# A macaron decoder layer: splitting the FFN's hidden tiles in the output projection, and 15 instead of 12 of 22 pairs as seven block products

## The chip, the cores and the metric

The kernel runs on one core of a Trainium2 chip. The metric is the device time of one execution in microseconds.

## The reference

One layer over 512 tokens of width 1024, all in float32, with four residual sub-layers in order: a half-step SwiGLU FFN, a token mixer (a gated delta rule and a sparse attention in parallel), a second half-step FFN, and a gated per-layer embedding. The change lies in the two FFNs, which compute

```
def swiglu(u, w_in, w_out):                  # u: 512 x 1024
    gate, up = split(u @ w_in, 2)            # w_in: 1024 x 5632, gate and up: 512 x 2816
    return (silu(gate) * up) @ w_out         # w_out: 2816 x 1024

h = h + 0.5 * rmsnorm(swiglu(rmsnorm(h, g_pre), w_in, w_out), g_post)
```

## The kernel before, in words

**Precision.** Each float32 operand is held as two tiles, a rounded hi part and a lo part (the value less its hi part). `mm3` (line 99) issues three matmuls for a product: hi x hi, hi x lo, lo x hi. A hi part is made by ScalarE (a cast), a lo part by VectorE (a subtraction). `wchunk` (line 83) loads a weight tile of 128 x 1024 through SP's queue and makes both parts; `parts` (line 282) does so for a tile that is already there.

**Input projection of an FFN** (`ffn`, line 384). The 2816 hidden channels are 22 tiles of 128 (f = 0 to 21), each with a gate and an up weight tile, a *pair*. The first pairs (f = 0 to 2 in the first FFN, 0 and 1 in the second) are done in two halves of 256 tokens by `start_tiles`. Of the rest, a *direct* pair makes two `pgu` tiles of 128 channels x 512 tokens: 8 steps over the width times 3 matmuls each, 48 matmuls of 512 columns. `ev` takes the gate through Silu (ScalarE, line 395), multiplies by up (VectorE, 398) and makes hid's hi and lo part (399, 400).

The other pairs go through `Seven.pair` (line 333): the pair is a 2 x 2 block product (gate and up by the two halves of the width, the two halves of the width by the two halves of the tokens) made with seven block products in place of eight, of the kind of Strassen and Winograd. The sums of token blocks are made once per FFN (`Seven.__init__`, after f = 3). For each pair VectorE makes sums of weight blocks (sa, sb; lines 339 to 343), `parts` splits three operands x1, x2, x3 of 128 x 1024 and one, x4, of 128 x 512, and TensorE does seven products of 12 matmuls of 256 columns: x1 twice, x2, x3, x2, x4, x3. They stand in four PSUM tiles (pfa, pfb, pfc, pfd), which lines 367 to 377 add up in the tile c; Silu (379), product (380) and the split into hid (382) follow.

The operands take turns in a ring of four slots (`ring`, line 320): three of the tags whi/wlo, and one, xr, at every fourth request. The raw weights take turns in four buffers (`load`, line 326), whether the pair is direct or not. x4, sa and sb have one buffer each.

Before, the pairs with f of at least 4 that are no multiple of 3 are sevens: 4, 5, 7, 8, ..., 19, 20, 12 in all, two at a time with a direct pair behind them.

**Output projection** (`out_proj`, line 188). Two halves of the output columns (ch), each with four accumulators (acc, one for each 128 tokens). For each half the loop runs over 11 weight tiles (j), each of which takes hid tiles 2j and 2j + 1: 4 x 2 x 3 matmuls of 512 columns. `load` (line 438) fetches the weights of j; the first two of ch = 0 take whi/wlo slots, the others the two buffers of vhi/vlo (which hold two of the sums of u before). The residual for the end (hr) is loaded on SP's queue into the buffer hz, which holds the other sums of u until the last seven.

**Order.** Each engine runs its instructions in an order fixed when the kernel is built: a scheduler simulates the program and gives each engine the ready instruction that stands first in the program. An engine can so be given work from further down the program when its buffers are free.

Of the kernel before, what the change touches and what calls it, by code (L numbers as in the profile page):

```python
# [7 lines left out]
F32 = mybir.dt.float32  # L8
F32R = mybir.dt.float32r
AF = mybir.ActivationFunctionType  # L10
ALU = mybir.AluOpType
# [4 lines left out]
T = 512  # L16
# [16 lines left out]
def layer_kernel(ctx, tc, x, pT, wf1, wo1, wfm, wsm, wtm, wbr, wout, wf2, wo2, wgate, wproj,  # L33
                 gains, consts, params, out):
    nc = tc.nc
    V, A, G, PE, SY = nc.vector, nc.scalar, nc.gpsimd, nc.tensor, nc.sync
# [4 lines left out]
    sp = ctx.enter_context(tc.tile_pool(name="sp", bufs=2))  # L41
# [14 lines left out]
    def mmp(name="mm"):  # L56
        return pp_.tile([128, 512], F32, name=name, tag="mm")

    def axp(name="ax"):
        return pp_.tile([128, 512], F32, name=name, tag="ax")  # L60
# [19 lines left out]
    def gain_row(i):  # L80
        return bass.AP(tensor=gains.tensor, offset=gains.offset + i * D, ap=[[0, 128], [1, D]])
# [17 lines left out]
    def mm3(ps, l, r, start, stop):  # L99
        PE.matmul(ps, l[0], r[0], start=start, stop=False)  # L100
        PE.matmul(ps, l[0], r[1], start=False, stop=False)  # L101
        return PE.matmul(ps, l[1], r[0], start=False, stop=stop)  # L102

    def cols(pair, a, b):
        return pair[0][:, a:b], pair[1][:, a:b]
# [7 lines left out]
    def new_u():  # L113
        return (up.tile([128, KT, T], F32R, name="uhi"), up.tile([128, KT, T], F32R, name="ulo"))

    def u_at(u, k, n):
        return u[0][:, k, n], u[1][:, k, n]
# [133 lines left out]
    def start_tiles(tiles, u):  # L251

        for si, n in enumerate(SEG):
            for i, (w, r, ev) in enumerate(tiles):
                ps = (mmp if si == 0 else axp)("p0")
                with in_order() if env.puts else ExitStack():
                    for k in range(KT):
                        m = mm3(ps[:r, n], cols(w, k * r, (k + 1) * r), u_at(u, k, n), k == 0, k == KT - 1)
                ev(n, ps)
                if si == 0 and i:  # L260
                    put(i + 1, m)
# [20 lines left out]
    def parts(dst, src):  # L282
        A.copy(dst[0], src)  # L283
        V.tensor_sub(dst[1], src, dst[0].bitcast(F32))
        return dst

    class Seven:
# [45 lines left out]
        def pair(self, f, wg, wu, hid):  # L333
            g, w = self.load(wg), self.load(wu)
            sa = env.small.tile([128, 1024], F32, name="sa", tag="gp")
            sb = env.small.tile([128, 1024], F32, name="sb", tag="gn")
            x4 = lp.tile([128, 1024], F32R, name="x4", tag="gx")
            x1 = parts(self.ring(), g)
            V.tensor_tensor(sa[:, H1], w[:, H1], w[:, H2], op=ALU.add)
            V.tensor_tensor(sa[:, H2], sa[:, H1], g[:, H1], op=ALU.subtract)  # L340
            x2 = parts(self.ring(), sa)
            V.tensor_tensor(sb[:, H1], g[:, H1], w[:, H1], op=ALU.subtract)
            V.tensor_tensor(sb[:, H2], g[:, H2], sa[:, H2], op=ALU.subtract)
            x3 = parts(self.ring(), sb)
            x4 = parts((x4[:, H1], x4[:, H2]), w[:, H2])
            N1, N2 = SEG

            def product(ps, x, c, b):
                for k in range(4):
                    mm3(ps, cols(x, c + k * 128, c + k * 128 + 128), b(k), k == 0, k == 3)  # L350

            def tb(i):
                return lambda k: (self.t[i][0][:, k], self.t[i][1][:, k])

            def ub(k0, n):
                return lambda k: u_at(self.u, k0 + k, n)

            def two(ps):
                return ps.rearrange("p (a b) -> p a b", b=256)

            def bc(a):
                return a[:, None, :].to_broadcast([128, 2, 256])

            c = self.fp.tile([128, 4, 256], F32, name=f"ct{f}", tag=f"hid{f}")
            pa, pb, pc, pd = mmp("pfa"), axp("pfb"), mmp("pfc"), axp("pfd")
            product(pa[:, N1], x1, 0, ub(0, N1))
            A.copy(c[:, 0], pa[:, N1])
            product(pb[:, N1], x1, 512, ub(4, N1))
            product(pb[:, N2], x2, 512, tb(1))
            V.tensor_tensor(c[:, 1:3], two(pb), bc(c[:, 0]), op=ALU.add)  # L370
            product(pc[:, N1], x3, 0, tb(2))
            product(pc[:, N2], x2, 0, tb(0))
            V.tensor_tensor(c[:, 0::3], two(pc), bc(c[:, 2]), op=ALU.add)
            V.tensor_tensor(c[:, 2], pc[:, N2], c[:, 0], op=ALU.add)
            product(pd[:, N1], x4, 0, tb(3))
            product(pd[:, N2], x3, 512, ub(4, N2))
            V.tensor_tensor(c[:, 0::3], two(pd), c[:, 0::3], op=ALU.add)
            t = sp.tile([128, 2, 256], F32, name="gt", tag="t512", bufs=2)
            A.activation(t, c[:, 1::2], AF.Silu)
            V.tensor_tensor(t, t, c[:, 0::2], op=ALU.mult)  # L380
            hid[f] = self.fp.tile([128, 2, T], F32R, name=f"hid{f}")
            parts((hid[f][:, 0], hid[f][:, 1]), t.rearrange("p a b -> p (a b)"))

    def ffn(fp, free, wf, wo, hsrc, u, gi, gn_i, first):
        hid = [None] * FT
        g = {}

        def ev(f, part):
            def run(n, ps):
                if part == 0:  # L390
                    if f == 2 and len(first) == 6:
                        t = g[f] = lp.tile([128, T + 608], F32, name="gx")
                    else:
                        t = g[f] = sp.tile([128, T], F32, name="gt", tag="t512", bufs=2)
                    A.activation(t[:, n], ps[:, n], AF.Silu)
                else:
                    t = g[f]
                    V.tensor_tensor(t[:, n], ps[:, n], t[:, n], op=ALU.mult)
                    A.copy(hid[f][:, 0, n], t[:, n])
                    V.tensor_sub(hid[f][:, 1, n], t[:, n], hid[f][:, 0, n].bitcast(F32))  # L400
            return run

        def hid_tile(f):
            return fp.tile([128, 2, T], F32R, name=f"hid{f}")

        nf = len(first) // 2
        for f in range(nf):
            hid[f] = hid_tile(f)
        start_tiles([(w, 128, ev(i // 2, i % 2)) for i, w in enumerate(first)], u)
        seven = None  # L410
        for f in range(nf, FT):
            if f >= 4 and f % 3:
                seven.pair(f, wf[2 * f], wf[2 * f + 1], hid)
                continue
            hid[f] = hid_tile(f)
            for i in range(2):
                if seven is None:
                    w = wchunk(wf[2 * f + i])
                else:
                    w = parts(seven.ring(), seven.load(wf[2 * f + i]))  # L420
                ps = mmp("pgu")
                for k in range(KT):
                    mm3(ps, cols(w, k * 128, (k + 1) * 128), u_at(u, k, ALL), k == 0, k == KT - 1)
                ev(f, i)(ALL, ps)
            if f == 3:
                seven = Seven(fp, u)

        h = hp.tile([128, 4, D], F32, name="hr", tag="hz")
        for tt in range(4):
            SY.dma_start(h[:, tt, :], hsrc(tt))  # L430
        gp = env.small.tile([128, D], F32, name="gp")
        gn = env.small.tile([128, D], F32, name="gn")
        SY.dma_start(gp, gain_row(gi))
        SY.dma_start(gn, gain_row(gn_i))
        ys = [env.small.tile([128, D], F32, name=f"ys{tt}") for tt in range(4)]
        u2 = new_u()

        def load(ch, j, a):
            dst = None
            if a is None:  # L440
                if ch or j > 1:
                    dst = upper(fp)
            else:
                dst = [fp.tile([128, 1024], F32R, name=f"xo{a}{i}", tag=f"hid{(14 + 2 * a if a < 4 else 0) + i}")
                       for i in range(2)]
            return wchunk(wo[ch, j], dst=dst)

        order2 = list(range(7, 11)) + list(range(0, 7))
        out_proj(11, load, lambda f, tk: (hid[f][:, 0, tk], hid[f][:, 1, tk]), list(range(11)), order2, 5, True,
                 ys, gp, sandwich_tail(h, ys, gn, u2), free)  # L450
        return h, u2
# [8 lines left out]
    with pool("s1", "right") as small:  # L460
        env.small = small
        f1_pool = ExitStack()
        fp = f1_pool.enter_context(pool("f1"))
# [649 lines left out]
    if True:  # L1113
# [9 lines left out]
        for m2 in range(4):  # L1123
            wb = wchunk(wbr[4 + m2], dst=upper(tl))
            for mi in range(2):
                m = 2 * m2 + mi
                py = (mmp if m < 4 else axp)("pya")
                for k in range(4):
                    c = mi * 512 + k * 128
# [4 lines left out]
                t = gate_load(m)  # L1134
# [23 lines left out]
    fp = f2_pool.enter_context(pool("f2"))  # L1158
# [126 lines left out]
```

## Time and profile before

| | us |
|---|---|
| median of 3 runs | 1294.93 |
| lowest and highest run | 1288.93, 1295.25 |
| the profiled execution | 1293.12 |
| its span in the profile | 1291.3 |
| TensorE (PE) busy | 1263.9 |
| VectorE (DVE) busy | 823.3 |
| ScalarE (ACT) busy | 522.6 |

All rows are of one profiled execution. Times within it count from the start of its span. PE is TensorE's matmuls, PEld its weight loads, SP the queue that issues the DMAs. The first FFN's input projection ends at 247.77 us, the second's at 1103.39 us. The ends of matmuls are modelled, so the pace of TensorE is read from the starts.

### The profile page before, as it was taken

The numbers are of one execution on the slowest core, as the hardware profiler recorded it, in microseconds if no ns is written. First come the engines' busy times: TensorE is split into PE (matmuls) and PEld (weight loads), VectorE is DVE, ScalarE is ACT, GpSimd is POOL, SyncE is SP. The second block draws the span as 40 slices with busy tenths as digits, with TensorE's granted clock in tenths as the row PEclk, the third lists the DMA queues.
The fourth block names the chain that finished last, engine by engine and source line by source line (L and its number), as shares of the span: only waits on it lengthen the run. The fifth ranks groups of instructions, "written<-read, shape, count | busy, mean of one in ns | idle before, by whom it ended". The sixth has DMA issues, their size and how long they took to land.

```text
span 1291.3 us, 18729 instructions
## 1 busy us (share of the span) xinstructions
PE 1263.9 (98%) x7525; PEld 1094.7 (85%) x7525; DVE 823.3 (64%) x1356; ACT 522.6 (40%) x845; POOL 65.3 (5%) x69
## 2 busy tenths in 40 slices
PE   6999999999999999999999999989999999999997
PEld 6999999888889888877678888769999999888876
DVE  6887777413372799986676454667777876123555
ACT  6444444312352543454655222344444444122353
POOL 0000000000010000030002011210000000000000
PEclk9999999999999999999999999999999999999999
DMA  6333333423542223335206635632433334223331
GB/s 220 101 98 103 110 99 115 163 71 95 153 148 88 68 68 114 98 111 144 67 6 146 208 117 170 212 113 76 132 108 105 101 115 133 99 94 113 114 114 66
DMA packets 59511, 147.69 MB, mean 114 GB/s; under 512 B 17760, under 2 KB 20256, under 8 KB 59424
## 3 DMA queue, kind: packets, MB, share of 16 engines
q1 hardware_dynamic: 58992, 144.93, 35.5%
q10 hardware_dynamic: 432, 1.57, 0.4%
q8 instruction: 59, 0.97, 0.3%
q14 instruction: 28, 0.23, 0.1%
HBM read 132.81 MB, written 13.66 MB: 113 GB/s over the span
## 4 chain that ended last, share of the span: by engine, by line
PE 86%; DMA 5%; DVE 5%; ACT 2%; issue 1%; POOL 0%; SPq 0%; DVEq 0%; POOLq 0%; ACTq 0%
PE acc L100 5%; PE acc L101 5%; PE acc L102 5%; PE pgu L101 4%; PE pgu L100 4%; PE pgu L102 4%; PE p L101 3%; PE p L102 3%; PE p L100 3%; PE ptm L100 2%; PE ptm L102 2%; PE ptm L101 2%; PE pg L100 2%; PE pg L102 2%; PE pg L101 2%; PE pfd L100 2%
## 5 line engine op out<-in xcount | busy, mean ns | idle before, releaser
L92 DVE TENSOR_TENSOR vlo<-raw,vhi 128x1024 fp32r<-128x1024 f32 x37 | 47.0, 1272 | 129.4 <-ACT vhi L91 129.3
L91 ACT CAST whi<-raw 128x1024 fp32r<-128x1024 f32 x70 | 73.6, 1051 | 125.7 <-PE pc L101 35.3
L92 DVE TENSOR_TENSOR wlo<-raw,whi 128x1024 fp32r<-128x1024 f32 x70 | 86.6, 1238 | 56.9 <-ACT whi L91 54.4
L102 PE MATMUL acc<-vhi,hid 128*128 128x512 f32 x240 | 93.4, 389 | 0.0
L101 PE MATMUL acc<-vlo,hid 128*128 128x512 f32 x240 | 93.4, 389 | 0.0
L91 ACT CAST vhi<-raw 128x1024 fp32r<-128x1024 f32 x37 | 38.7, 1048 | 131.4 <-PE acc L102 115.9
L100 PE MATMUL acc<-vhi,hid 128*128 128x512 f32 x240 | 81.7, 389 | 0.0
L78 POOL TENSOR_TENSOR rinv<-ms,mhalf 128x1 f32<-128x1 f32 x32 | 19.3, 605 | 819.7 <-DVE ms L123 819.7
L100 PE MATMUL pgu<-uhi,whi 128*128 128x512 f32 x144 | 56.2, 390 | 0.0
L101 PE MATMUL pgu<-ulo,whi 128*128 128x512 f32 x144 | 56.2, 390 | 0.0
L102 PE MATMUL pgu<-uhi,wlo 128*128 128x512 f32 x144 | 56.0, 389 | 0.0
L100 PEld LDWEIGHTS acc<-vhi,hid 128*128 128x128 f32 x240 | 45.1, 188 | 9.4
L101 PEld LDWEIGHTS acc<-vlo,hid 128*128 128x128 f32 x240 | 45.0, 188 | 9.4
L102 PEld LDWEIGHTS acc<-vhi,hid 128*128 128x128 f32 x240 | 45.0, 188 | 9.4
L101 PE MATMUL ptm<-wlo,uhi 128*128 128x512 f32 x128 | 50.3, 393 | 0.0
L100 PE MATMUL ptm<-whi,uhi 128*128 128x512 f32 x128 | 50.0, 395 | 0.0
L102 PE MATMUL ptm<-whi,ulo 128*128 128x512 f32 x128 | 49.8, 391 | 0.0
L283 ACT CAST whi<-sb 128x1024 fp32r<-128x1024 f32 x24 | 25.2, 1049 | 53.0 <-PE pfc L101 38.6
L100 PE MATMUL pg<-uhi,whi 128*128 128x512 f32 x104 | 41.2, 396 | 0.0
L102 PE MATMUL pg<-uhi,wlo 128*128 128x512 f32 x104 | 40.9, 393 | 0.0
L100 PE MATMUL pc<-uhi,whi 128*128 128x512 f32 x96 | 38.2, 398 | 2.6 <-ACT DT L803 2.6
L101 PE MATMUL pg<-ulo,whi 128*128 128x512 f32 x104 | 40.7, 392 | 0.0
(519 smaller groups left out, 3918.3 us busy)
## 6 DMA issues: line engine op xcount, KB each, us to landing
raw<-wf SPq DMA_DIRECT2D x52, 512.0 KB, 3.9
raw<-wo SPq DMA_DIRECT2D x44, 512.0 KB, 3.6
rawy<-wf SPq DMA_DIRECT2D x36, 512.0 KB, 3.7
raw<-wfm SPq DMA_DIRECT2D x28, 512.0 KB, 3.7
raw<-wtm SPq DMA_DIRECT2D x20, 512.0 KB, 3.6
gd<-gst SPq DMA_DIRECT2D x16, 256.0 KB, 2.0
raw<-wbr SPq DMA_DIRECT2D x8, 512.0 KB, 4.0
grl<-gd SPq DMA_DIRECT2D x16, 256.0 KB, 3.8
```

Of the source, the lines that this page charges most:

```text
L78: G.tensor_tensor(out_, in_, e, op=ALU.pow)
L91: A.copy(hi[:, :n], raw[:, :n])
L92: (eng or V).tensor_sub(lo[:, :n], raw[:, :n], hi[:, :n].bitcast(F32))
L100: PE.matmul(ps, l[0], r[0], start=start, stop=False)
L101: PE.matmul(ps, l[0], r[1], start=False, stop=False)
L102: return PE.matmul(ps, l[1], r[0], start=False, stop=stop)
L283: A.copy(dst[0], src)
```

## The change

Three things change. The threshold and pattern for sevens: f of at least 5 with f mod 6 other than 4, so 5 to 9, 11 to 15 and 17 to 21, 15 in all. The tile that a pair leaves behind is no longer hid's hi and lo part but the plain float32 product, in the same memory: in the second and fourth quarter of c for a seven, in the first half of the tile for a direct pair. And the hi and lo parts are made by a new function `split`, called by the output projection's `load` for the tiles 2j and 2j + 1 when the weights of j are loaded for ch = 0: a copy to a tile t (one of two buffers, shared with Silu's results), then the cast and the subtraction into a new tile in the old one's memory.

```diff
@@ -377,9 +377,8 @@
             V.tensor_tensor(c[:, 0::3], two(pd), c[:, 0::3], op=ALU.add)
             t = sp.tile([128, 2, 256], F32, name="gt", tag="t512", bufs=2)
             A.activation(t, c[:, 1::2], AF.Silu)
-            V.tensor_tensor(t, t, c[:, 0::2], op=ALU.mult)
-            hid[f] = self.fp.tile([128, 2, T], F32R, name=f"hid{f}")
-            parts((hid[f][:, 0], hid[f][:, 1]), t.rearrange("p a b -> p (a b)"))
+            V.tensor_tensor(c[:, 1::2], t, c[:, 0::2], op=ALU.mult)
+            hid[f] = c
@@ -395,13 +394,11 @@
                     t = g[f]
-                    V.tensor_tensor(t[:, n], ps[:, n], t[:, n], op=ALU.mult)
-                    A.copy(hid[f][:, 0, n], t[:, n])
-                    V.tensor_sub(hid[f][:, 1, n], t[:, n], hid[f][:, 0, n].bitcast(F32))
+                    V.tensor_tensor(hid[f][:, 0, n], ps[:, n], t[:, n], op=ALU.mult)
             return run
 
         def hid_tile(f):
-            return fp.tile([128, 2, T], F32R, name=f"hid{f}")
+            return fp.tile([128, 2, T], F32, name=f"ct{f}", tag=f"hid{f}")
@@ -409,7 +406,7 @@
         for f in range(nf, FT):
-            if f >= 4 and f % 3:
+            if f >= 5 and f % 6 != 4:
                 seven.pair(f, wf[2 * f], wf[2 * f + 1], hid)
                 continue
@@ -435,7 +432,17 @@
+        def split(f):
+
+            t = sp.tile([128, 2, 256], F32, name="gt", tag="t512", bufs=2)
+            A.copy(t, hid[f][:, 1::2] if hid[f].shape[1] == 4 else hid[f][:, 0].rearrange("p (a b) -> p a b", b=256))
+            hid[f] = fp.tile([128, 2, T], F32R, name=f"hid{f}")
+            parts((hid[f][:, 0], hid[f][:, 1]), t.rearrange("p a b -> p (a b)"))
+
         def load(ch, j, a):
+            if ch == 0:
+                split(2 * j)
+                split(2 * j + 1)
             dst = None
```

## Rows read from the trace of the kernel before

**Rows 1.** The page: span, busy time by engine, chain of waits.

```profile
span 1291.3 us, 18729 instructions
...
PE 1263.9 (98%) x7525; PEld 1094.7 (85%) x7525; DVE 823.3 (64%) x1356; ACT 522.6 (40%) x845; POOL 65.3 (5%) x69
...
PE 86%; DMA 5%; DVE 5%; ACT 2%; issue 1%; POOL 0%; SPq 0%; DVEq 0%; POOLq 0%; ACTq 0%
```

**Rows 2.** Waits of TensorE, whole span, the first and last of nine: us, times, longest.

```profile
PE put L108 <- DVE ys L132: 7.5, 1, 7.5
...
PE p L101 <- DVE ms L123: 0.8, 1, 0.8
```

**Rows 3.** Windows (us, busy PE, PEld, DVE, ACT, POOL; clock, DMA): f=3, 7, 8, 9, both projections.

```profile
52.70:63.61 10.91, 10.91 (x51) 9.02 (x49) 5.79 (x8) 2.69 (x6) 0.00 (x0) 1.00 0.35 103
94.29:104.23 9.94, 9.94 (x85) 9.93 (x84) 6.95 (x9) 4.64 (x6) 0.00 (x0) 1.00 0.16 54
104.23:114.03 9.80, 9.80 (x87) 9.80 (x86) 8.75 (x13) 5.08 (x7) 0.00 (x0) 1.00 0.51 162
114.03:124.99 10.96, 10.96 (x51) 9.02 (x49) 8.22 (x12) 3.88 (x6) 0.00 (x0) 1.00 0.27 96
52.70:247.77 195.07, 195.07 (x1346) 181.51 (x1345) 145.49 (x194) 84.92 (x113) 0.00 (x0) 1.00 0.35 114
897.44:1103.39 205.95, 205.95 (x1395) 190.52 (x1393) 157.56 (x208) 91.69 (x120) 0.00 (x0) 1.00 0.37 120
```

**Rows 4.** Instructions of the tile pfa: min, median, max ns, first and last start.

```profile
L100 PE MATMUL pfa<-uhi,whi x48: 277/283/283, 63.6 to 1073.8; 128*128 128x256 f32 x48
L100 PE MATMUL pfa<-uhi,xr x48: 276/276/276, 73.5 to 1083.6; 128*128 128x256 f32 x48
```

**Rows 5.** Timeline of VectorE, 94 to 121 us: start, us, what [idle before].

```profile
102.31 0.42 DVE L374 TENSOR_TENSOR ct<-pfc,ct 128x256 f32<-128x256 f32 x1
102.65 1.22 DVE L284 TENSOR_TENSOR wlo<-sb,whi 128x1024 fp32r<-128x1024 f32 x1
103.78 0.68 DVE L284 TENSOR_TENSOR x<-raw,x 128x512 fp32r<-128x512 f32 x1
...
108.00 0.69 DVE L339 TENSOR_TENSOR sa<-raw 128x512 f32<-128x512 f32 x1 [0.74 <-DMA raw<-wf]
...
117.76 0.68 DVE L339 TENSOR_TENSOR sa<-rawy 128x512 f32<-128x512 f32 x1
118.47 0.69 DVE L340 TENSOR_TENSOR sa<-sa,rawy 128x512 f32<-128x512 f32 x1
119.08 0.69 DVE L284 TENSOR_TENSOR hid<-gt,hid 128x512 fp32r<-128x512 f32 x1
```

**Rows 6.** Timeline of VectorE, at the first two sevens of the first FFN.

```profile
78.21 0.69 DVE L339 TENSOR_TENSOR sa<-rawy 128x512 f32<-128x512 f32 x1 [1.62 <-DMA rawy<-wf]
```

**Rows 7.** Timeline of TensorE: the first matmul on x3 in f=8.

```profile
108.37 0.28 PE L100 MATMUL pfc<-vhi,whi 128*128 128x256 f32 x1
```

**Rows 8.** Groups by line and form: the cast of hid in sevens, whole span.

```profile
L283 ACT CAST hid<-gt 128x512 fp32r<-128x512 f32 x24 | 14.8, 617 | 11.5 <-DVE gt L380 11.5
```

**Rows 9.** Groups by line and form: weights in the output projection, 247.77 to 320 us.

```profile
L91 ACT CAST vhi<-raw 128x1024 fp32r<-128x1024 f32 x11 | 11.5, 1048 | 53.6 <-PE acc L102 53.6
L92 DVE TENSOR_TENSOR vlo<-raw,vhi 128x1024 fp32r<-128x1024 f32 x11 | 13.5, 1225 | 48.4 <-ACT vhi L91 48.4
```

**Rows 10.** Chain of waits, 262 to 300 us: start, us; one step of j apart.

```profile
270.05 0.91 PE acc L100 x4
275.49 0.91 PE acc L100 x4
```

**Rows 11.** Timelines of SP and ScalarE at the end of the input projection.

```profile
235.57 2.47 SPq L430 DMA_DIRECT2D hr<-x  x4
238.14 10.85 SPq L85 DMA_DIRECT2D raw<-wo  x4
...
245.10 1.05 ACT L91 CAST vhi<-raw 128x1024 fp32r<-128x1024 f32 x1 [2.04 <-DMA raw<-wo]
```

## The prediction

> **What bounds the kernel now.** I read the page first. TensorE is busy for 98% of the span, the vector engine for 64%, the scalar engine for 40%, and the chain of waits runs over TensorE for 86% of the span [rows 1]. So a change of the time must come out of TensorE's own work or out of a new gap in it. The list of TensorE's waits then says where gaps are today: nine entries, and every one is at a transposition, at the start of a stage, at the mixer or at the end; none is in the tiles of the FFN's input projection (pgu, pfa to pfd) [rows 2]. The windows confirm it: over both input projections TensorE is busy for the whole window, at a granted clock of 1.00, its 2.4 GHz level [rows 3]. The part the change touches is therefore paced by TensorE's instruction stream, and the question is how much of it goes and whether the other engines still keep up.
>
> **The price of a pair.** The window edges are the starts of a pair's first matmul. A direct pair (48 matmuls of 512 columns) takes 10.91 us with both weights in the whi/wlo slots and 10.96 with one in the xr slot; a seven-product pair (84 matmuls of 256 columns) takes 9.94 us with all weights in whi/wlo and 9.80 with its first in xr [rows 3]. That last difference is in the matmuls: those on xr weights are 276 ns long, those on whi 283 [rows 4]. Check: one FFN has 6 sevens at 9.94, 6 at 9.80, 6 direct at 10.96 and f=3 at 10.91, which makes 195.1; the window has 195.07 [rows 3].
>
> **The change, part 1: three more pairs as seven products in each FFN.** Afterwards f=3, 4, 10, 16 are direct (f=2 too in the second FFN) and 15 are sevens. Counting the ring (every fourth request is xr) from f=4: f=16 gets one xr, the other direct pairs none, 11 sevens have one xr, and in 4 of these it is the first operand. Direct: 3 x 10.91 + 10.96 = 43.69. Sevens: if xr helps only as first operand, 4 x 9.80 + 11 x 9.94 = 148.5; if it helps in every place, 11 x 9.80 + 4 x 9.94 = 147.6. No row shows xr as second or third operand; I take the middle, 148.05, since both ends are equally near. Sum 191.74 against 195.07: 3.33 us less per FFN (2.8 to 3.8), **6.7 us for two (5.7 to 7.6)**. The Trainium skill, "TensorE: Matmul & The Clock Gate", section "Back-to-back issue gap", gives a matmul its columns over 2.4 GHz plus 2.5 ns; by it a direct pair would be 10.36 us, a seven 9.17 and the gain 7.1 us. The windows show both slower than that rule, so the rows are used.
>
> **Part 2: the vector engine's load in a run of sevens.** In the second of two sevens VectorE runs without idle from 108.00 to 119.68 us: 17 instructions, of which 13 are of 512 elements, 3 of 1024 and one of 256; the next one starts 0.60, 1.14 and 0.34 us after such a one (118.47 to 119.08, 102.65 to 103.78, 102.31 to 102.65) [rows 5]. A seven has 10, 3 and 1 of these: 9.76 us. The change takes one of 512 out (the lo part of hid): 9.16. TensorE needs 9.80 to 9.94, so a run of five just fits, at 93%. Two things eat into the 0.7 us left. An instruction that uses the result of the one just ahead starts 0.71 instead of 0.60 later (117.76 to 118.47). And the first addition of a pair's up weight waited 0.74 us for its DMA [rows 5], in another place 1.62 [rows 6]; that load can only start once the x4 split has freed its buffer, so the wait comes back in each pair. With one of each, 9.16 + 0.11 + 0.74 = 10.0: over TensorE's 9.84 by 0.2 a pair, 0.9 us over five. That is covered by the lead: the third operand's lo part was done at 103.87 and first used at 108.37 [rows 5, 7], 4.5 us. The direct pair behind a run needs only 2 x 1.14 + 0.60 = 2.9 us of VectorE in 10.9, so the lead is won back. I cost this at **nothing**; if the cover goes, each 0.1 us a seven goes over costs 0.5 us in a run of five, of which there are three per FFN.
>
> ScalarE drops the cast of hid here too (0.62 us each); in the busier window it is busy 5.08 of 9.80 us [rows 3]. PSUM is no tighter: a pair uses two of four banks in each group. The number and order of weight loads on SP's queue is the same, since every pair from f=4 on takes its two loads from the same ring of four buffers, direct or not.
>
> **Part 3: seven starts one pair later.** The sums of u that the products need (13 vector instructions of 1024) are made after f=3 and now have f=4's 10.9 us as cover as well. The list of waits shows no gap there before. Nothing.
>
> **Part 4: splits in the output projection.** Each of 44 tiles now costs a copy (new, priced like the 512 cast beside it, 0.62), a cast (0.62, moved) and a subtraction (0.68, moved) [rows 5, 8]. Per j that is 2.5 us of ScalarE and 1.4 of VectorE, beside the weight's own 1.05 and 1.23 [rows 9]: 3.5 and 2.6 us in a step of 5.44 us of TensorE [rows 10]. Even with splits and weight in series, 3.5 + 1.23 = 4.8 is under 5.44. At the first step the splits of f=0 and 1 need only tiles finished some 190 us earlier, and ScalarE is half idle. The first weight takes the slot of f=21's first operand, free 7 us ahead of the projection, and needs 2.3. **Nothing**; if neither split were done when TensorE arrives, 4 x 0.62 + 0.68 = 3.2 us per FFN.
>
> **Part 5: the residual's load.** The buffer for hr is freed by the sixth of a pair's products. The last seven is f=21 instead of f=20, so this comes 1.4 us ahead of the output projection instead of 12. On SP's queue the four hr loads stand ahead of four weight loads; the first of these was cast 9.5 us after the queue got free (235.57 to 245.10) [rows 11]. If that order stays, the third weight is ready 1.4 us less than 9.5 + 2.3 into the projection, at 10.4; it is used two steps in, at 10.9. Just covered. Its raw buffer comes free before hr's, so it may also go ahead. Nothing, with little to spare.
>
> **The sum.** 6.7 us off. The profiled execution took 1293.12 us, of which 1291.3 is the span; it would be 1286.4. It stands 1.8 us under the median of the three runs (1294.93), which are 6 us apart, so against the median: **1288.3 us**, 0.5% less. About 0.5% (6.5 us) is what a measurement of this kernel can tell from no change, and the forecast lies on that line.
>
> **Rivals.**
> - *VectorE sets the pace in the runs of five.* If instructions take their full lengths (0.68, 1.22, 0.42 us) a seven takes 9 x 0.68 + 3 x 1.22 + 0.42 = 10.2 us, and with the long DMA wait of 1.62 [rows 6] 11.9. That is 2.0 over TensorE; five make 10, less 4.5 of lead 5.6, times six runs 33: **1321 us**. It decides from 0.9 us over per seven on; a slowdown past 0.5% needs 1.3. For it: VectorE is at 93% and its order is fixed beforehand, so an instruction that waits holds all behind it. Against it: in the trace the starts stand 0.60 apart where the lengths are 0.68, and a wait for TensorE vanishes once VectorE is late.
> - *Full lengths, and the short DMA wait.* 10.2 + 0.74 = 11.0, 1.1 over; five make 5.7, less 4.5, times six is 7: **1295 us**. Against it: the starts stand 0.60 apart where the lengths are 0.68 [rows 5]. The Trainium skill, "VectorE: DVE Perf Modes", section "The DRAIN you can't avoid", says for it that the next operation starts only when the pipe is empty; by that rule each would cost its full length, and the trace does not agree.
> - *The hand-over costs what the pairs give.* The splits of the first step or hr's transfers leave TensorE waiting 3.2 us at the head of both output projections: 6.3 of 6.7 us go back, **1294.6 us**. For it: 0.5 us to spare in part 5, and the splits are last in the program. Against it: ScalarE's idle half.
> - *The new operand places of xr gain nothing or all*: 1289.2 or 1287.3; inside the forecast.
>
> **How the numbers follow.** TensorE paces throughout: 0.72, divided by the 0.5% line into 0.42 faster and 0.30 same, as the estimate is just past it and losses can only take from it. Hand-over: 0.13, same. Full lengths: 0.04, same. VectorE's pace: 0.11, slower. Range: the lowest run shown, 1288.93, less 6.7 gives 1282; upward through the hand-over, the full lengths and the small end of the VectorE case, 1299; the rest of that case is left out.
>
> **What would show it.** Pairs as now: 9.8 to 9.95 us for each seven, five in a row some 49.3 us, TensorE busy through the window, 191.7 for the first FFN; no wait at pfa to pfd in the list; 30 copies of pfa instead of 24; VectorE's window near 93%; the splits' casts spread over the input projection or the first steps of the output projection, with steps of 5.44. The forecast is wrong if TensorE waits in the fourth or fifth seven for a lo part, if acc waits for hid, or if matmuls on xr weights in other places are slower than on whi.

## The result, and the profile after

The changed kernel takes 1300.1 us in the median of six runs (1299.01 to 1301.4), the kernel before 1293.22 in six runs on the same chip (1288.93 to 1295.25): a ratio of 1.0056 [1.004, 1.0071], slower by about 7 us. The forecast of 1288.3 us had the wrong sign, and the time lies above its range. The profiled execution took 1300.13 us with a span of 1298.3 (before 1293.12 and 1291.3). A few executions of the kernels below run some 30 to 45 us longer at a lower granted clock; medians and ratios leave them out, and the traces of e4 and e5 are of such executions, with both FFNs in them at a clock of 1.00.

The page of the kernel after, its span and its first part (answers to [rows 1]):

```profile
span 1298.3 us, 19333 instructions
...
PE 1262.9 (97%) x7741; PEld 1105.0 (85%) x7741; DVE 863.2 (66%) x1411; ACT 559.8 (43%) x902; POOL 66.3 (5%) x69
```

TensorE is busy for 1262.9 us, 1.0 less than before, in a span that is 7.0 longer: the pairs gave something, and TensorE stands still for longer. The waits of TensorE after, whole span, the first two of twelve entries (waited for: us, times, longest; answers to [rows 2]):

```profile
PE acc L100 <- ACT hid L283: 8.2, 2, 4.9
PE put L108 <- DVE ys L132: 7.1, 1, 7.1
```

The first entry is new: the output projection (acc) waits for a hi part of hid, once in each FFN, 4.9 and 3.3 us. No entry names pgu or pfa to pfd, as before. So the input projection itself still runs without a gap. The windows after show what it gained and what followed (columns as in [rows 3]): the five sevens f = 5 to 9 together, four of them one by one, the first FFN's input projection from its first pgu to the first acc, the gap, and the start of the output projection, in both FFNs.

```profile
75.42:125.12 49.70, 49.70 (x421) 49.70 (x420) 43.68 (x60) 22.80 (x29) 0.00 (x0) 1.00 0.33 106
85.40:95.35 9.95, 9.95 (x86) 9.95 (x85) 9.22 (x14) 4.68 (x6) 0.00 (x0) 1.00 0.33 105
95.35:105.33 9.98, 9.98 (x86) 9.98 (x85) 9.13 (x13) 4.67 (x6) 0.00 (x0) 1.00 0.32 107
105.33:115.13 9.80, 9.80 (x87) 9.80 (x85) 8.61 (x13) 4.68 (x6) 0.00 (x0) 1.00 0.33 109
115.13:125.12 9.99, 9.99 (x86) 9.99 (x85) 9.07 (x14) 4.65 (x6) 0.00 (x0) 1.00 0.49 157
53.63:251.35 197.72, 192.82 (x1454) 185.03 (x1453) 154.89 (x209) 81.94 (x105) 0.00 (x0) 0.99 0.33 106
246.31:249.30 2.99, 0.14 (x2) 0.00 (x0) 1.65 (x2) 1.04 (x1) 0.00 (x0) 1.00 0.94 347
249.30:256.10 6.80, 4.75 (x11) 3.78 (x12) 3.64 (x6) 6.46 (x11) 0.00 (x0) 0.50 0.77 302
256.10:261.50 5.40, 5.40 (x24) 4.33 (x24) 3.73 (x5) 4.94 (x10) 0.00 (x0) 1.00 0.29 97
1109.50:1112.90 3.40, 3.22 (x8) 2.54 (x9) 2.08 (x3) 3.31 (x7) 0.00 (x0) 0.50 1.01 386
```

Three things are to be read. Five sevens in a row take 49.70 us with TensorE busy throughout and VectorE for 43.68. TensorE is busy for 192.82 of the 197.72 us up to the first acc. And the granted clock, 1.00 up to the gap, stands at 0.50, the 1.2 GHz level, from 3.0 us into the gap until 256.10, and again for 3.4 us in the second FFN.

Stage by stage, from TensorE's starts (us; the input projection runs from the first pgu to the first acc, the output projection from there to the first put, the transposition behind it):

| stage | before | after | difference |
|---|---|---|---|
| up to the first pgu | 52.70 | 53.63 | +0.93 |
| first FFN, input projection | 195.07 | 197.72 | +2.65 |
| first FFN, output projection | 115.02 | 116.87 | +1.85 |
| from there to the second FFN's first pgu | 534.65 | 534.47 | -0.18 |
| second FFN, input projection | 205.95 | 207.00 | +1.05 |
| second FFN, output projection | 114.61 | 116.15 | +1.54 |
| from there to the end of the span | 73.3 | 72.5 | -0.8 |

The four stages of the FFNs make 7.1 of the 7.0 us. (The first stage begins with the first loads; it ends between 51.95 and 53.91 us in the traces of all kernels here, whatever the change. The first output projection of before takes 115.02 us, 0.4 more than its second, because its first put waits for another tile.)

The chain of waits after, at the hand-over of the first FFN (start us, us, what):

```profile
241.66 4.89 DMA raw<-wo
...
246.57 1.05 ACT vhi L91
...
247.65 0.04 DVE vlo L92
247.69 1.11 issue
248.79 0.69 DVE ct L377
...
249.51 0.63 ACT gt L379
250.14 0.52 ACT gt L438
...
250.68 0.63 ACT hid L283
...
251.35 0.79 PE acc L100
252.14 0.43 PE acc L101
```

TensorE's last matmul of pair 21 starts at 246.17. What follows is a row of small steps in series: the last sum of the pair's PSUM tiles (L377), its Silu (L379), and only then the *first* copy of a split (L438), its cast (L283) and the first acc. That sum is itself 2.3 us late: ahead of it on VectorE stands the lo part of the third weight (vlo), which waits for its cast and that for its transfer. The timeline of ScalarE at the same place (start us, us, line, operation; in brackets the idle time before and its releaser):

```profile
239.32 1.05 ACT L91 CAST whi<-raw 128x1024 fp32r<-128x1024 f32 x1 [1.00 <-PE pfb L101]
243.57 1.05 ACT L91 CAST whi<-raw 128x1024 fp32r<-128x1024 f32 x1 [3.20 <-PE pfc L101]
246.57 1.04 ACT L91 CAST vhi<-raw 128x1024 fp32r<-128x1024 f32 x1 [1.95 <-DMA raw<-wo]
249.51 0.63 ACT L379 ACTIVATE gt<-ct 128x512 f32<-128x512 f32 x1 [1.89 <-DVE ct L377]
250.05 0.60 ACT L438 COPY gt<-ct 128x512 f32<-128x512 f32 x1
```

ScalarE idles for 1.00, 3.20, 1.95 and 1.89 us and does not use any of it for the copies of f = 0 and 1, whose data has been there for 190 us. The copy starts right behind pair 21's Silu. This suggests a buffer: Silu's result and a split's copy share the two buffers of the tag t512. If these are given out in the order of the program, the first split can have one only when pair 21 has taken its own, which a seven does at its very end.

### The profile page after: what moved, and what is told of

Same layout as the page of the kernel before. It is cut to its first block, busy times and chain, and to the rows that moved or that the text cites. A ratio compares the mean times of both kernels' runs of the same rounds, so it can differ in the third digit from the quotient of the medians.

```text
span 1298.3 us, 19333 instructions
## 1 busy us (share of the span) xinstructions
PE 1262.9 (97%) x7741; PEld 1105.0 (85%) x7741; DVE 863.2 (66%) x1411; ACT 559.8 (43%) x902; POOL 66.3 (5%) x69
## 4 chain that ended last, share of the span: by engine, by line
PE 87%; DMA 5%; DVE 4%; ACT 2%; issue 1%; SPq 0%; POOL 0%; DVEq 0%; POOLq 0%; ACTq 0%
PE acc L100 7%; PE acc L101 7%; PE acc L102 7%; PE p L101 3%; PE p L102 3%; PE p L100 3%; PE pgu L101 3%; PE pgu L100 3%; PE pgu L102 3%; PE ptm L100 2%; PE ptm L101 2%; PE ptm L102 2%; PE pfb L100 2%; PE pfb L101 2%; PE pfb L102 2%; PE pfd L100 2%
## 5 line engine op out<-in xcount | busy, mean ns | idle before, releaser
L283 ACT CAST whi<-sb 128x1024 fp32r<-128x1024 f32 x24 | 25.2, 1048 | 76.9 <-PE pfc L101 42.1
L101 PE MATMUL pgu<-ulo,whi 128*128 128x512 f32 x128 | 49.9, 390 | 0.0
L100 PE MATMUL pgu<-uhi,whi 128*128 128x512 f32 x128 | 49.9, 390 | 0.0
L102 PE MATMUL pgu<-uhi,wlo 128*128 128x512 f32 x128 | 49.8, 389 | 0.0
L284 DVE TENSOR_TENSOR hid<-gt,hid 128x512 fp32r<-128x512 f32 x44 | 29.0, 689 | 19.7 <-ACT hid L283 19.7
```

## The experiments

The theory: the loss is at the hand-over and comes from the order of these buffers, with the wait of VectorE and the low clock behind it. The rivals: that the new pattern of sevens or the deferral costs time by itself; that the late transfers of weights and hr make the gap; and that the splits come last because they are last in the program. In the table is the median of each kernel, its ratio to the kernel before in the same runs, and the two projections of the first FFN together (first pgu to put, from the starts in its trace; before 310.09, after 314.59). The medians differ by more than the FFNs do: the stretch between the two FFNs alone takes 531.91 to 538.33 us in the traces other than those of e4 and e5, with no pattern by the change.

| kernel | us | ratio [95%] | first FFN, us |
|---|---|---|---|
| e1: new pattern, splits as before | 1291.28 | 0.997 [0.9957, 0.9983] | 307.27 |
| e2: deferred splits, old pattern | 1293.65 | 0.9996 [0.9984, 1.0007] | 309.67 |
| e3: change, f = 0 to 3 split at once | 1289.29 | 0.9963 [0.9949, 0.9977] | 307.27 |
| e4: change, first four splits moved ahead | 1286.93 | 0.9949 [0.9935, 0.9963] | 307.27 |
| e5: change, pair 21's Silu in another buffer | 1288.89 | 0.9961 [0.9949, 0.9974] | 307.27 |
| e6: change, vlo behind pair 21 | 1299.29 | 1.0037 [1.0022, 1.0051] | 311.48 |
| e7: e4 with 17 sevens | 1288.96 | 0.9957 [0.9943, 0.9972] | 305.39 |
| e8: 17 sevens, splits as before | 1287.15 | 0.9939 [0.9925, 0.9953] | 305.28 |
| e9: e8, xr always the first operand | 1283.81 | 0.9914 [0.9894, 0.9935] | 303.49 |
| e10: e7, xr always the first operand | 1285.53 | 0.9927 [0.9905, 0.9948] | 303.77 |
| e11: e10 with 18 sevens | 1278.82 | 0.9883 [0.9864, 0.9902] | 301.92 |
| e12: e9 with 18 sevens | 1279.23 | 0.9892 [0.9873, 0.9912] | 302.51 |

### The two halves of the change alone

e1, the kernel before with the new pattern only:

```diff
-            if f >= 4 and f % 3:
+            if f >= 5 and f % 6 != 4:
```

> The kernel before with the new pattern of sevens (5 to 9, 11 to 15, 17 to 21) and hid still split in its pair. Theory A (the changed kernel lost its time at the hand-over to the output projection: 5.2 and 3.6 us of gap and some 4 us at half clock behind them, while the pairs gained 2.3 us per FFN): no gap at the hand-over, clock 1.00 there, about 4.6 us less than before (ratio 0.9965). Rival B (the deferral is needed, as VectorE cannot keep up with five sevens in a row): gaps at pfa to pfd in the fourth or fifth seven, ratio 1.000 or above.

e2, the kernel after with the old pattern:

```diff
-            if f >= 5 and f % 6 != 4:
+            if f >= 4 and f % 3:
```

> The changed kernel with the old pattern (two sevens and a direct pair; f=21 direct). Theory A, with the cause that the splits take their tiles t from the two buffers of Silu's results in program order: f=21's Silu of the gate comes 5 us before its end, so split 0 can be made ahead, split 1 must wait for f=21's product: a gap of 1.5 to 3 us at each hand-over, time 2 to 6 us over before (ratio 1.002 to 1.005). Rival C (the gap belongs to the chain behind a last pair made of sevens alone): gap under 0.5 us, ratio 1.000.

e1 is faster than before, with no wait at the hand-over: its input projections take 192.66 and 203.54 us, 2.41 less in each FFN. So the pattern alone gains, and the splits made at once do not hold it back. VectorE is the busier for them, as the window of e1 over nearly the same stretch shows, but TensorE does not wait:

```profile
75.42:125.12 49.70, 49.70 (x422) 49.70 (x421) 45.39 (x63) 25.32 (x34) 0.00 (x0) 1.00 0.34 106
```

e2 costs nothing either: 0.9996, the input projection at 195.07 us as before, no gap. A gap of 1.5 to 3 us had been expected here, and this miss explains most. The timeline of ScalarE in e2 at its hand-over:

```profile
241.77 0.60 ACT L394 ACTIVATE gt<-pgu 128x512 f32<-128x512 f32 x1 [4.02 <-PE pgu L102]
242.26 0.62 ACT L438 COPY gt<-ct 128x512 f32<-128x512 f32 x1
242.91 0.62 ACT L283 CAST hid<-gt 128x512 fp32r<-128x512 f32 x1
...
246.24 0.61 ACT L438 COPY gt<-ct 128x512 f32<-128x512 f32 x1
```

In the old pattern f = 21 is a direct pair. Its gate is finished in the middle of the pair, so Silu takes its t512 buffer at 241.77, more than 4 us ahead of the output projection. The first copy follows at once, though all splits stand later in the program than all of pair 21. The expectation had the second copy wait for pair 21's product; it starts at 246.24, ahead of that product (249.58), so the one buffer that Silu left over served both splits. So neither half costs anything alone; the loss needs both: deferred splits *and* a seven as last pair.

### Taking the buffer out of the way

e3, the kernel after, but hid of f = 0 to 3 is split at once in `ev`, as before, and `load` splits only for j > 1:

```diff
...
+                    if f > 3:
+                        V.tensor_tensor(hid[f][:, 0, n], ps[:, n], t[:, n], op=ALU.mult)
+                        return
+                    V.tensor_tensor(t[:, n], ps[:, n], t[:, n], op=ALU.mult)
+                    A.copy(hid[f][:, 0, n], t[:, n])
+                    V.tensor_sub(hid[f][:, 1, n], t[:, n], hid[f][:, 0, n].bitcast(F32))
...
-            if ch == 0:
+            if ch == 0 and j > 1:
```

> The changed kernel, but hid of f=0 to 3 is split where it is made, as in the kernel before; the other 18 are split in the output projection. Theory A: no gap at the hand-over and no half clock behind it; ratio 0.9965, 12 us less than the changed kernel. Rival D (the splits as such slow the first steps, as ScalarE and VectorE cannot feed them): gaps or steps over 5.5 us at j=2 to 5, ratio 1.000 or above.

e4, the kernel after with the first four splits called ahead of pairs 20 and 21 (`split` is defined further up; `load` splits only for j > 1):

```diff
+            if f >= 20:
+                split(2 * f - 40)
+                split(2 * f - 39)
             if f >= 5 and f % 6 != 4:
...
-            if ch == 0:
+            if ch == 0 and j > 1:
```

> The changed kernel with the calls of the first four splits moved in the program: those of f=0, 1 ahead of pair 20, those of f=2, 3 ahead of pair 21. Same instructions, buffers and copies. Theory A: the place in the program is the cause, the splits are done before the last pair ends: no gap, ratio 0.9965 as e3. Rival E (the scheduler puts them last for another reason, or copy and cast are slow wherever they stand): the gap stays over 3 us, ratio over 1.003.

e5, the kernel after with one thing changed: pair 21's Silu result goes into x4's buffer instead of t512:

```diff
-            t = sp.tile([128, 2, 256], F32, name="gt", tag="t512", bufs=2)
+            if f == 21:
+                t = lp.tile([128, 2, 256], F32, name="gu", tag="gx")
+            else:
+                t = sp.tile([128, 2, 256], F32, name="gt", tag="t512", bufs=2)
```

> The changed kernel with one buffer changed: the Silu result of pair 21 goes to the buffer of x4 (free by then) instead of one of the two that the splits' tiles share. All calls stay where they are in the program. Theory A (the splits stand behind pair 21 because it has to take its buffer first): the first splits are made before the last pair ends, no gap, no half clock at the hand-over, ratio 0.995 to 0.997. Rival F (the place in the program as such, not the buffer): gaps of 5 and 3.5 us stay, ratio 1.005.

All three remove the gap and the low clock, and all three come to the same 307.27 us as e1. e3 and e4 leave open whether it was the buffer or the place in the program. e5 settles it: the splits stand where the change put them. The timeline of ScalarE in e5 (first FFN; L441 is the split's copy, L382 the Silu of a seven, of pair 20 in the first row and of pair 21 in the last but one):

```profile
237.19 0.63 ACT L382 ACTIVATE gt<-ct 128x512 f32<-128x512 f32 x1 [1.47 <-DVE ct L377]
237.72 0.61 ACT L441 COPY gt<-ct 128x512 f32<-128x512 f32 x1
...
239.02 0.63 ACT L441 COPY gt<-ct 128x512 f32<-128x512 f32 x1
...
248.94 0.63 ACT L382 ACTIVATE gu<-ct 128x512 f32<-128x512 f32 x1
249.47 0.61 ACT L283 CAST hid<-gt 128x512 fp32r<-128x512 f32 x1
```

The first copy is now made at 237.72, right behind pair 20's Silu, 12 us earlier than in the change and 11 ahead of pair 21's Silu. So the place in the program did not by itself hold the splits back, and the buffer did: a split has its turn behind the last Silu that takes a t512 buffer ahead of it in the program. That Silu is pair 21's in the change, the first half of the direct pair 21 in e2 and pair 20's in e5. In e4, where the split of f = 0 is called ahead of pair 20, it is pair 19's:

```profile
228.55 0.63 ACT L379 ACTIVATE gt<-ct 128x512 f32<-128x512 f32 x1
229.09 0.61 ACT L406 COPY gt<-ct 128x512 f32<-128x512 f32 x1
```

### The wait of VectorE

e6, the kernel after with the third weight's load and parts issued behind pair 21's product:

```diff
-            V.tensor_tensor(c[:, 1::2], t, c[:, 0::2], op=ALU.mult)
+            self.last = V.tensor_tensor(c[:, 1::2], t, c[:, 0::2], op=ALU.mult)
...
-            return wchunk(wo[ch, j], dst=dst)
+            with (tc.issue_after(seven.last.ins) if (ch, j) == (0, 2) else ExitStack()):
+                return wchunk(wo[ch, j], dst=dst)
```

> The changed kernel with the parts of the third output weight issued after pair 21's product, so that VectorE's lo part of it no longer stands ahead of the last pair's sums. Theory A (this and the late DMA are a share of the gap; the rest is the chain sum, Silu, copy, cast): gaps fall from 5.2 and 3.6 to about 3.0 and 2.4 us, ratio 1.001 to 1.004. Rival G (the order on VectorE costs nothing, the chain is the whole gap): gaps stay, 1.005.

The waits of TensorE in e6, the entry of the hand-over:

```profile
PE acc L100 <- ACT hid L283: 5.2, 2, 2.6
```

and two windows of e6 behind its gaps:

```profile
248.10:251.60 3.50, 3.15 (x8) 2.53 (x9) 2.29 (x4) 3.30 (x7) 0.00 (x0) 0.52 0.99 394
1108.20:1111.70 3.50, 3.50 (x10) 2.70 (x9) 2.29 (x5) 3.07 (x6) 0.00 (x0) 0.51 1.00 391
```

What stays is 2.6 us in each FFN: sum 0.69, Silu 0.63, copy 0.52 and cast 0.63 make 2.5. What went is 2.3 us in the first FFN (4.9 to 2.6) and 0.7 in the second (3.3 to 2.6): that was VectorE standing at vlo. So the late transfer makes a gap longer and does not open it: in e5 it stands where it stood, and there is no gap. The clock falls to about half behind these shorter gaps as well, and the output projections still take 116.06 and 116.24 us instead of 114.6.

### What is to be had from here

With the gap gone, three questions were left: does VectorE keep up without any direct pair among the sevens, does the deferral then pay, and what is xr worth?

e7, e4 with `f >= 5` as the only condition, 17 sevens in a row:

```diff
-            if f >= 5 and f % 6 != 4:
+            if f >= 5:
```

> The kernel of e4 with every pair from f=5 on as a seven, 17 in a row. Theory A (VectorE keeps up with deferred splits: 10.0 us a seven against 9.95, covered by the lead): no gap, 0.96 us less for each of 4 more pairs, about 3.8 us less than e4, ratio 0.992. Rival B (VectorE sets the pace in a long run): gaps or late operands from about the tenth seven on, ratio 0.996 or above.

e8, the kernel *before* with the same 17 sevens, each split in its own pair:

```diff
-            if f >= 4 and f % 3:
+            if f >= 5:
```

> The kernel before, hid split in its pair, with every pair from f=5 on as a seven. Theory A: VectorE has 9.76 us and its waits for 9.95 us of TensorE; if it is over by 0.4 a pair, 17 pairs make 7 us, less 4.5 of lead: 2 to 3 us of gaps per FFN, ratio 0.996 to 0.999. Rival H (waits vanish when VectorE is late, so it keeps pace at 9.8): no gaps, ratio 0.993, and then nothing in the input projection needed the deferral.

Both go from 307.27 to 305.4 and 305.3 us: each direct pair made a seven gives 0.9 to 1.0 us, and the deferral nothing. The rest of e7's expected median (0.992) did not come; its pace in the FFNs did. For e8 theory A, with gaps, was wrong, and rival H came true. In e8 the scheduler mixes the matmuls of neighbouring pairs from about the tenth seven on and lets some acc matmuls start between those of the last pair, which is why the two projections are compared together.

e9 is e8, and e10 is e7, with xr given to every seven's first operand, and only to that:

```diff
-        def ring(self):
-            self.n[0] += 1
-            if self.n[0] % 4 == 0:
+        def ring(self, first=False):
+            if first:
...
-            x1 = parts(self.ring(), g)
+            x1 = parts(self.ring(True), g)
```

> The kernel of e8 (17 sevens, hid split in its pair) with the xr slot given to the first operand of every seven and the three whi slots to the others. Theory A (xr helps as first operand, 276 against 283 ns a matmul, and not elsewhere): sevens of 9.80 us, some 2 us less per FFN than e8 from the start of f=3 to the first transposition behind the output projection (305.3 there), ratio 0.990. Rival B (VectorE, 9.76 us and its waits, now sets the pace): matmuls still waiting or out of order, under 1 us less per FFN, ratio 0.993.

> The kernel of e7 (17 sevens, splits deferred, the first four moved ahead of the last pairs) with the same use of xr. Theory A: 2 us less per FFN than e7 (305.4 for the same stretch), ratio 0.991 to 0.993; VectorE has 9.16 us for 9.80 and does not bind. Rival I (the single xr buffer comes too late for the next pair): gaps at pfa.

e9 gains 1.8 us in each FFN over e8. e10 gains 2.2 us in each input projection over e7 (188.40 against 190.65 us, 199.28 against 201.53); in the first FFN 1.6 of it are left, as a later put waits there. The forms of TensorE's matmuls at line 100, the first of the three of a product, first in the kernel after and then in e9 (x1 is the operand of pfa and of pfb with uhi, x2 of pfb with vhi, x2 again of pfc with t; ns least/median/most):

```profile
L100 PE MATMUL pfa<-uhi,whi x44: 277/283/285, 75.4 to 237.4; 128*128 128x256 f32 x44
L100 PE MATMUL pfb<-vhi,whi x44: 277/281/284, 88.3 to 240.3; 128*128 128x256 f32 x44
L100 PE MATMUL pfc<-t,whi x44: 277/279/283, 91.1 to 243.1; 128*128 128x256 f32 x44
L100 PE MATMUL pfb<-vhi,xr x16: 280/282/286, 78.3 to 220.3; 128*128 128x256 f32 x16
L100 PE MATMUL pfc<-t,xr x16: 279/285/286, 81.1 to 223.1; 128*128 128x256 f32 x16
```

```profile
L100 PE MATMUL pfa<-uhi,xr x68: 276/276/282, 75.6 to 231.5; 128*128 128x256 f32 x68
L100 PE MATMUL pfc<-t,whi x68: 277/278/283, 81.3 to 241.9; 128*128 128x256 f32 x68
```

xr shortens the matmuls of the first operand (276 against 283 ns). It lengthens those of the second at this line (282 against 281, 285 against 279); at lines 101 and 102 they differ by 1 ns at most. In e9 and e10 13 of the 17 sevens get xr as first operand for the first time. From e7 to e10 12 of them go from between 9.95 and 10.00 us to 9.80, and the first, behind a direct pair, from 9.99 to 9.93: together some 2.2 us, the gain of e10's input projection. In e9 and e12 the matmuls of neighbouring pairs are mixed as in e8, and e9 gains less.

e11 and e12 add f = 4 to e10 and e9:

```diff
-            if f >= 5:
+            if f >= 4:
```

> The kernel of e10 with f=4 as a seven too, 18 in all. Theory A: 1.1 us less per FFN than e10, ratio 0.990 to 0.992. Rival J (the sums of u are not ready when the first seven follows f=3 at once): a gap at the first pfb of each FFN, no gain.

> The kernel of e11 without any deferral: 18 sevens, xr for the first operands, hid split in its pair. Theory A (deferring the splits gains nothing even at the fastest pace, VectorE keeps up at 9.76 us): 301.9 us from f=3 to the transposition behind the output projection as in e11, ratio 0.988. Rival B (with no direct pair left to catch up, VectorE falls behind): over 303 us for that stretch, ratio 0.991 or above.

Both are about 1.1% faster than the kernel before, 1278.82 and 1279.23 us, and their intervals cover each other. The window of e12 over 140 us of sevens in a row:

```profile
64.00:204.00 140.00, 140.00 (x1198) 139.92 (x1198) 132.20 (x188) 72.28 (x98) 0.00 (x0) 1.00 0.30 100
```

VectorE is at 94% with each split made in its pair, and TensorE never waits. e12 was expected to take the 301.9 us of e11 in the first FFN; it takes 302.51, and 0.6 us more in the second FFN too. So the half of the change that defers the splits gives 0.6 us in each FFN at this pace, which the medians can't tell from nothing; 18 sevens in a row run without it.

## Why the prediction was wrong

**Part 4, the splits, is the step that failed.** It said that "the splits of f=0 and 1 need only tiles finished some 190 us earlier, and ScalarE is half idle". Both are true and neither decides: a split also needs a t512 buffer, and its turn for one comes behind pair 21's Silu. I had read in the code that t shares its two buffers with Silu's results and had not asked in what order they are given out. Part 5 had noted that the last seven becomes f = 21, but only for hr's load: a seven's Silu comes after all its matmuls, where the direct f = 21 of before took its buffer in the middle of the pair (e2). Costed at nothing, the place cost, start to start, 5.06 and 3.45 us beyond a normal step (5.18 and 3.57 less 0.12), of which 2.3 and 0.7 belong to VectorE's wait at vlo (e6).

**The clock was no term at all.** Behind the gaps the first acc matmuls start 0.43 us apart, as in the chain above, at a granted clock of 0.50; a step of 24 in 5.40 us, 0.23 each, follows at 1.00. Against 114.61 us the output projections lost 2.26 and 1.54 us by it. The Trainium skill, "TensorE: Matmul & The Clock Gate", section "Back-to-back issue gap", puts matmuls of N columns N over 1.2 GHz apart at the lower level; an estimate by it for 512 columns is 0.427 us, and the trace's 0.43 agrees. In e3, e4 and e5, which take the gap away, the low clock is gone too.

**Part 1, the pairs, was right in kind and mis-sized.** The three more sevens gave 2.41 us in each FFN instead of 3.33, under the low end of 2.8. Of "xr helps only as first operand" and "in every place" the first is nearer, and the seven without it costs more than the 9.94 I used: the windows above show 9.80 for the one with x1 in xr, 9.95 for one with x3 there, 9.99 for one with x2 there and 9.98 for one with none. Two more windows after, of f = 11 (x1 in xr) and f = 17 (none), both right behind a direct pair:

```profile
136.03:145.95 9.92, 9.92 (x85) 9.92 (x84) 7.64 (x10) 4.15 (x5) 0.00 (x0) 1.00 0.18 54
196.63:206.57 9.94, 9.94 (x85) 9.93 (x84) 7.65 (x10) 4.14 (x5) 0.00 (x0) 1.00 0.17 54
```

Before, every seven without xr stood right behind a direct pair, and there the 9.94 still holds; behind another seven it does not, and x1 in xr does not always give 9.80. With the direct pairs as I priced them, 15 sevens take 192.66 - 43.69 = 148.97 us; less 3 x 9.80 and 9.92 that is 9.97 for each of the other 11.

**The account:** gaps 5.06 + 3.45, low clock 2.26 + 1.54, together 12.3; less 2 x 2.41 from the pairs, 7.5 us; less the 0.4 that before lost at its first put, 7.1. The span grew by 7.0, the median by 6.9.

**Parts 2, 3 and 5 were right.** VectorE keeps up with five sevens in a row (43.68 of 49.70 us, 88%, where I had put 93%), and e8 and e12 show 17 and 18 in a row with the split in each pair. The first of the five starts without a wait, and pgu has none. hr's load does not hold up the output projection: e5, which leaves the load where it was, runs 114.61 us there. A weight load does stand late, but it was the order on VectorE that made it cost something.

**The rivals.** "The hand-over costs what the pairs give" named the right place at 0.13, with 3.2 us for each FFN, if "neither split were done when TensorE arrives". That was the case, but the price left out the pair's own sum and Silu in the chain, the 2.3 us of VectorE behind a transfer, and the clock; the measured loss is 7.3 and 5.0. VectorE as the pace and the full instruction lengths did not happen. The Trainium skill, "VectorE: DVE Perf Modes", section "The DRAIN you can't avoid", which the rival of the full lengths names, also says that a next operation which is not held starts earlier; the starts 0.60 us apart at lengths of 0.68 [rows 5] agree with that. Of the signs named, "if acc waits for hid" came true, and in part "if matmuls on xr weights in other places are slower than on whi": x2's first matmuls with t take 285 ns on xr and 279 on whi, though a pair with x2 in xr (9.98 and 9.99 us) is no slower than one with none (9.98).

## What to carry to other kernels

When work is moved to a later place in the program, list not only its data but every buffer it takes and who takes that buffer ahead of it: a new buffer user behind the last unit of the old loop inherits that unit's finish, however idle its engine is. At the hand-over between the two phases here a gap of 2.6 to 4.9 us cost another 1.5 to 2.3 us by the clock behind it, so a term for the clock belongs in the sum. And before work is deferred to relieve an engine, try the denser order without it: here e12 ran without it at 0.6 us more in each FFN.

## What was not expected of the hardware

The granted clock fell to 0.50 while TensorE had been idle for only a few us, and it stayed there after work had begun again: 6.8 us of it with a gap of 4.9 us, 3.4 us with one of 3.3, and about as long with the gaps of 2.6 in e6. The pace of the same 256-column matmul depends on which tile holds its operand and against which tokens it runs: 276 ns for x1 in xr, 283 for x1 in whi, 279 for x2 in whi against t and 285 for x2 in xr. The tile is not all of it, since f = 11 with x1 in xr takes 9.92 us and f = 8 takes 9.80. What makes the difference was not tried; giving the slots to operands by these rows was worth 1.8 us in each FFN in e9 and 2.2 in each input projection in e10.
